# A sliding-window copy: staging whole batches or inner blocks in pairs

## The chip, the cores and the metric

The kernel runs on one core of a Trainium2 chip. The metric is device time in microseconds (us), the median of the timed runs of one program. The kernel before takes 755.48 us, the median of three runs from 754.17 to 756.32. The profiled execution is one more run, with a span of 749.4 us between its first and its last instruction.

## The reference

The kernel computes nothing. It copies overlapping windows of its input.

```python
batch, length, dim = (32, 4096, 256)
window_size = 64
stride = 32

def reference(x, window_size, stride):
    n_windows = (length - window_size) // stride + 1        # 127
    result = np.zeros((batch, n_windows, window_size, dim), dtype=np.float32)
    for i in range(n_windows):
        start = i * stride
        result[:, i] = x[:, start:start + window_size].copy()
    return result
```

A window has twice as many rows as the stride. So it helps to think in *blocks* of 32 rows, 32 x 256 x 4 bytes = 32 KB each. A batch has 128 blocks, and window w is block w followed by block w + 1, that is 64 KB. Block b therefore appears twice in the output: as the first half (half 0) of window b and as the second half (half 1) of window b - 1. Only block 0 and block 127 appear once. The input is 134.2 MB and the output 266.3 MB.

## The kernel before

There are two ways to make a window. A *direct* copy goes from DRAM to DRAM and reads 64 KB for a 64 KB window, so every block is read twice. A *staged* copy loads each block once into on-chip memory (SBUF) and stores it twice. Staging saves reads of DRAM, but moves three blocks' worth of bytes through the DMA engines where direct copying moves two. The kernel uses both at once. SyncE issues direct copies, ScalarE issues loads and stores of staged items, and GpSimd[...] issues remainders near the end.

```python
DIRECT, IN, OUT = 32768, 16384, 16384       # largest piece of a transfer, bytes

class Copier:
    def windows(self, q, b, w0, n, half=None, piece=DIRECT):
        blk = self.blk                       # one block, in elements
        row = [1, 2 * blk if half is None else blk]
        h = half or 0
        return q.dma_start(
            out=self.oap((b * self.nw + w0) * 2 + h, [[2 * blk, n], row]),
            in_=self.xap(b * self.nb + w0 + h, [[blk, n], row]),
            max_dma_last_dim=piece,
        )
    # ... columns: n windows cut into 16 parts each; load, store: blocks to and from a tile

class Staging:                               # cut: __init__ with six tiles of 128 x 32 KB
    def load(self, q, g):
        i = g % len(self.tiles)
        b, c, n = self.items[g]
        if self.count[self.stored[i]]:
            q.wait_ge(self.stored[i], self.count[self.stored[i]])
        step = 128 // n
        parts = [(k, 4, 32, 1) for k in range(4)] if g == 0 else [(0, step, n, step)]
        for rows in parts:
            self.issue(self.c.load(q, self.tiles[i], b, c, rows), self.loaded[i])
        # ...
    def store(self, q, g):
        # ... waits for loaded[i]; one store of all 128 blocks for half 0, one for half 1
        parts, end = [((0, step, n, step), 0), ((0, step, n, step), 1)], []
        # ... the last item is cut into smaller stores, counted in `ended`
    def run(self, q):                        # six loads, six stores, five loads, five stores
        # ...
```

The eleven staged items are whole batches of 128 blocks, one block to a partition. A store of such an item for half 1 puts block 0 of batch b into the second half of the last window of batch b - 1, where it doesn't belong, and a store for half 0 puts block 127 into the first half of a window of the next batch. The direct copies of the neighbouring batches write these places again. They have to come later, so those *edges* wait for the staged stores.

```python
    staged = [*range(1, B, 3)]
    items = [(b, -1 if b == B - 1 else 0, c.nb) for b in staged]
    direct = [b for b in range(B) if b not in staged]
    # ...
    sixteens = []
    for b in direct:
        w = 15 if b - 1 in staged else 0
        sixteens += [(b, w + 16 * j) for j in range((c.nw - w) // 16)]
    edges = [(b, 0 if b - 1 in staged else 112, 15) for b in direct[:-1]]
    last = B - 2
    edges.append((last, 112, 4))

    first_loads, loads, stores = 6 * 17, 5 * 17, 6 * 34
    turns = share = 0
    with tc.tile_critical():
        st.run(ring_s)
        for i, (b, w) in enumerate(sixteens):
            # ...
            second = turns - first_loads - stores
            loading = turns < first_loads or 0 <= second < loads
            share += 120 if turns < 16 or -8 <= second < 16 else 90 if loading else 18
            if share >= 120:                 # one transfer of 16 windows as two of 16 halves
                share -= 120
                turns += 4
                count(c.windows(ring_d, b, w, 16, 0), done)
                count(c.windows(ring_d, b, w, 16, 1), sem)
            else:
                turns += 3
                count(c.windows(ring_d, b, w, 16), sem)
        # ...
        ring_r.wait_ge(near, 16)
        for b, w, n in edges:
            for k in (b - 1, b + 1):
                if k in place and b != last:
                    st.wait_stored(ring_r, place[k])
            count(c.windows(ring_r, b, w, n), rest)
        # ... the last windows, cut in columns, and the waits for everything
```

The variable `turns` counts packets and completions per DMA engine. A transfer of 16 windows gives each of 16 engines one window of 64 KB, which is two pieces of 32 KB and a completion, 3 turns. In two halves it is 4 turns. With `share` the code sets how many turns the SyncE ring has against the ScalarE ring.

Of the kernel before, what the change touches and what calls it, by code (L numbers as in the profile page):

```python
# [8 lines left out]
DIRECT, IN, OUT = 32768, 16384, 16384  # L9


class Copier:


    def __init__(self, x, out, B, L, D, W, S, n_win):
        assert W == 2 * S and L % S == 0
        self.x, self.out = x, out
        self.B = B
        self.blk = S * D
        self.nb = L // S  # L20
        self.nw = n_win

    def xap(self, block, dims):
        return bass.AP(self.x.tensor, self.x.offset + block * self.blk, dims)

    def oap(self, half_window, dims):
        return bass.AP(self.out.tensor, self.out.offset + half_window * self.blk, dims)

    def windows(self, q, b, w0, n, half=None, piece=DIRECT):

        blk = self.blk
        row = [1, 2 * blk if half is None else blk]
        h = half or 0
        return q.dma_start(  # L34
            out=self.oap((b * self.nw + w0) * 2 + h, [[2 * blk, n], row]),
            in_=self.xap(b * self.nb + w0 + h, [[blk, n], row]),
            max_dma_last_dim=piece,
        )

    def columns(self, q, b, w0, n):  # L40

        part = self.blk // 8
        row = [1, part]
        return q.dma_start(  # L44
            out=self.oap((b * self.nw + w0) * 2, [[part, 16], [2 * self.blk, n], row]),
            in_=self.xap(b * self.nb + w0, [[part, 16], [self.blk, n], row]),
        )

    def load(self, q, t, b, c, rows):

        p, step, n, unit = rows
        return q.dma_start(
            out=t[p : p + (n - 1) * step + 1 : step, :],
            in_=self.xap(b * self.nb + c + p // unit, [[step // unit * self.blk, n], [1, self.blk]]),
            max_dma_last_dim=IN,
        )

    def store(self, q, t, b, c, rows, half):


        p, step, n, unit = rows
        w = b * self.nw + c + p // unit - half
        return q.dma_start(
            out=self.oap(2 * w + half, [[2 * step // unit * self.blk, n], [1, self.blk]]),
            in_=t[p : p + (n - 1) * step + 1 : step, :],
            max_dma_last_dim=OUT,
        )


class Staging:  # L70


    def __init__(self, c, tc, pool, dtype, items, bufs):
        self.c, self.items = c, items
        self.tiles = [pool.tile([128, c.blk], dtype, name=f"xb{i}") for i in range(bufs)]
        self.loaded = [tc.alloc_semaphore(f"loaded{i}") for i in range(bufs)]
        self.stored = [tc.alloc_semaphore(f"stored{i}") for i in range(bufs)]
        self.ended = tc.alloc_semaphore("ended")
        self.count = {sem: 0 for sem in (*self.loaded, *self.stored, self.ended)}
        self.after_load, self.after_store = {}, {}  # L80

    def issue(self, dma, sem):
        dma.then_inc(sem, 16)
# [1 line left out]

    def load(self, q, g):
        i = g % len(self.tiles)
        b, c, n = self.items[g]
        if self.count[self.stored[i]]:
            q.wait_ge(self.stored[i], self.count[self.stored[i]])  # L90
        step = 128 // n
        parts = [(k, 4, 32, 1) for k in range(4)] if g == 0 else [(0, step, n, step)]
        for rows in parts:
            self.issue(self.c.load(q, self.tiles[i], b, c, rows), self.loaded[i])
        self.after_load[g] = self.count[self.loaded[i]]

    def store(self, q, g):
        i = g % len(self.tiles)
        b, c, n = self.items[g]
        q.wait_ge(self.loaded[i], self.after_load[g])  # L100
        step = 128 // n
        parts, end = [((0, step, n, step), 0), ((0, step, n, step), 1)], []
        if g == len(self.items) - 1:

            parts = [((0, 1, 128, 1), 1), ((0, 1, 32, 1), 0)]
            end = [(96, 1, 32, 1)] + [(32 + k, 4, 16, 1) for k in range(4)]
        for rows, half in parts:
            self.issue(self.c.store(q, self.tiles[i], b, c, rows, half), self.stored[i])
        for rows in end:
            self.issue(self.c.store(q, self.tiles[i], b, c, rows, 0), self.ended)  # L110
        self.after_store[g] = self.count[self.stored[i]]

    def wait_stored(self, q, g):
        q.wait_ge(self.stored[g % len(self.tiles)], self.after_store[g])  # L114

    def run(self, q):
        bufs = len(self.tiles)
        for first in range(0, len(self.items), bufs):
            group = range(first, min(first + bufs, len(self.items)))
            for g in group:  # L120
                self.load(q, g)
            for g in group:
                self.store(q, g)


@with_exitstack
def kernel(
    ctx: ExitStack,
    tc: tile.TileContext,
    x: bass.AP,  # L130
    window_size: bass.AP,
    stride: bass.AP,
    out: bass.AP,
):
    nc = tc.nc
    W, S = int(window_size), int(stride)
    B, L, D = x.shape
    n_win = (L - W) // S + 1
    assert out.shape == (B, n_win, W, D)
    c = Copier(x, out, B, L, D, W, S, n_win)  # L140


    staged = [*range(1, B, 3)]
    items = [(b, -1 if b == B - 1 else 0, c.nb) for b in staged]
    place = {b: g for g, (b, _, n) in enumerate(items) if n == c.nb}
    direct = [b for b in range(B) if b not in staged]
    pool = ctx.enter_context(tc.tile_pool(name="xb", bufs=1))
    st = Staging(c, tc, pool, x.dtype, items, 6)
    ring_d, ring_s, ring_r = nc.sync, nc.scalar, nc.gpsimd
    done = tc.alloc_semaphore("done")  # L150
    near = tc.alloc_semaphore("near")
    rest = tc.alloc_semaphore("rest")
    total = {done: 0, near: 0, rest: 0}

    def count(dma, sem):
        dma.then_inc(sem, 16)
        total[sem] += 16

    sixteens = []
    for b in direct:
        w = 15 if b - 1 in staged else 0
        sixteens += [(b, w + 16 * j) for j in range((c.nw - w) // 16)]
    singles = [(B - 1, c.nw - 1, 1)]
    edges = [(b, 0 if b - 1 in staged else 112, 15) for b in direct[:-1]]
    last = B - 2
    edges.append((last, 112, 4))

    first_loads, loads, stores = 6 * 17, 5 * 17, 6 * 34  # L170
    turns = share = 0
    with tc.tile_critical():  # L172
        st.run(ring_s)

        for i, (b, w) in enumerate(sixteens):
            sem = near if i == len(sixteens) - 2 else done
            second = turns - first_loads - stores
            loading = turns < first_loads or 0 <= second < loads
            share += 120 if turns < 16 or -8 <= second < 16 else 90 if loading else 18
            if share >= 120:  # L180
                share -= 120
                turns += 4
                count(c.windows(ring_d, b, w, 16, 0), done)
                count(c.windows(ring_d, b, w, 16, 1), sem)
            else:
                turns += 3
                count(c.windows(ring_d, b, w, 16), sem)
            if i == len(sixteens) // 2:
                for b, w, half in singles:
                    count(c.windows(ring_d, b, w, 1, half, 2048), done)  # L190

        ring_r.wait_ge(near, 16)
        for b, w, n in edges:
            for k in (b - 1, b + 1):
                if k in place and b != last:
                    st.wait_stored(ring_r, place[k])
            count(c.windows(ring_r, b, w, n), rest)


        count(c.columns(ring_r, last, 116, 9), rest)  # L200
        st.wait_stored(ring_d, place[B - 1])
        count(c.columns(ring_d, last, 125, 2), done)
        total[st.ended] = st.count[st.ended]
        for sem, n in total.items():
            ring_d.wait_ge(sem, n)


# [33 lines left out]
```

## Time and profile before

| | before |
|---|---|
| time, median of 3 (us) | 755.48 |
| span of the profiled execution (us) | 749.4 |
| loads issued by ScalarE | 10 of 4096 KB, 4 of 1024 KB |
| stores issued by ScalarE | 21 of 4096 KB, 2 of 1024 KB, 4 of 512 KB |
| direct copies issued by SyncE | 92 of 1024 KB, 110 of 512 KB, 1 of 128 KB, 1 of 32 KB |
| direct copies issued by GpSimd | 20 of 960 KB, 1 of 576 KB, 1 of 256 KB |
| median from issue to landing, SyncE's 1024 KB copies (us) | 100.7 |
| median from issue to landing, ScalarE's 4096 KB stores (us) | 139.7 |

The profile of such a kernel is read from its DMA side. A row of 40 slices shows how busy the sixteen DMA engines were in each fortieth of the span (a digit is tenths, 9 is 90% or more) and how many GB/s they moved. A table of queues gives each ring's packets, bytes and the share of the sixteen engines' time that its packets took. Stretches of the span can also be asked for one by one. The long times from issue to landing are no latency of the hardware: a transfer is issued while others still stand ahead of it on its ring.

### The profile page before, as it was taken

The page shows a single profiled execution, that of the slowest core. Times are in us where ns is not written, and L with a number is a line of the kernel's source. Part 1 is how long each engine was busy: PE and PEld are TensorE (multiplying, and loading weights), DVE is VectorE, ACT ScalarE, POOL GpSimd, SP SyncE. Part 2 cuts the span into 40 slices and gives each one's busy share as a digit, 9 for nine tenths or more (in the row PEclk, how much of TensorE's full clock was granted, in tenths as well). Part 3 has the DMA queues.
Part 4 walks back from the last instruction along what each step waited for, and adds up shares of the span by engine and source line. Part 5 has one row for each costly group of instructions (what it writes and reads, how often), then busy time and mean ns, then how long its engine had stood idle before and what let it go on. Part 6 is the DMA issues. An engine that isn't in the chain of part 4 may idle for free.

```text
span 749.4 us, 322 instructions
## 1 busy us (share of the span) xinstructions
POOL 12.8 (2%) x26
## 2 busy tenths in 40 slices
POOL 0000000000000000000000000000000000040100
DMA  8999999999999999999999999999999999999996
GB/s 360 401 427 429 427 429 428 434 423 418 420 424 423 418 424 415 422 427 427 414 427 417 429 432 429 430 422 430 429 423 421 423 421 419 425 426 423 431 409 262
DMA packets 18290, 313.26 MB, mean 418 GB/s; under 512 B 4336, under 2 KB 4336, under 8 KB 4528
## 3 DMA queue, kind: packets, MB, share of 16 engines
q1 hardware_dynamic: 8016, 154.32, 48.8%
q10 hardware_dynamic: 9104, 138.41, 44.0%
q0 software_dynamic: 1168, 20.51, 6.5%
q14 instruction: 2, 0.02, 0.0%
HBM read 220.95 MB, written 267.09 MB: 651 GB/s over the span
## 4 chain that ended last, share of the span: by engine, by line
another core or an unknown queue 92%; POOL 2%; issue 0%; POOLq 0%; SPq 0%
POOL out_dram L34 2%; POOL out_dram L44 0%; POOLq L236 0%; SPq L172 0%; POOLq L114 0%
## 5 line engine op out<-in xcount | busy, mean ns | idle before, releaser
L34 POOL DMA_DIRECT2D out_dram<-in_x_dram x21 | 12.0, 576 | 691.3 <-DMA out_dram<-in_x_dram 654.0
L44 POOL DMA_DIRECT2D out_dram<-in_x_dram x1 | 0.6, 581 | 0.0
L222 POOL MEMSET const-float32-0.0<- 128x1 f32 x1 | 0.1, 98 | 0.2 <-issue 0.2
L222 POOL MEMSET const-bfloat16-1.0<- 128x1 bf16 x1 | 0.1, 101 | 0.0
L222 POOL MEMSET const-float32-1.0<- 128x1 f32 x1 | 0.1, 98 | 0.0
L222 POOL MEMSET const-uint8-127<- 128x1 uint8 x1 | 0.1, 98 | 0.0
## 6 DMA issues: line engine op xcount, KB each, us to landing
out_dram<-in_x_dram SPq DMA_DIRECT2D x92, 1024.0 KB, 100.7
out_dram<-xb ACTq DMA_DIRECT2D x21, 4096.0 KB, 139.7
out_dram<-in_x_dram SPq DMA_DIRECT2D x110, 512.0 KB, 90.3
xb<-in_x_dram ACTq DMA_DIRECT2D x10, 4096.0 KB, 131.4
out_dram<-in_x_dram POOLq DMA_DIRECT2D x20, 960.0 KB, 38.5
xb<-in_x_dram ACTq DMA_DIRECT2D x4, 1024.0 KB, 15.7
out_dram<-xb ACTq DMA_DIRECT2D x2, 1024.0 KB, 113.4
out_dram<-xb ACTq DMA_DIRECT2D x4, 512.0 KB, 96.9
```

The lines of the kernel that those rows point to most:

```text
L34: return q.dma_start(out=self.oap((b * self.nw + w0) * 2 + h, [[2 * blk, n], row]), in_=self.xap(b * self.nb + w0 + h, [[blk, n], row]), m ...
L44: return q.dma_start(out=self.oap((b * self.nw + w0) * 2, [[part, 16], [2 * self.blk, n], row]), in_=self.xap(b * self.nb + w0, [[part, 16 ...
L222: nc = _bacc.Bacc("TRN2", target_bir_lowering=False, num_devices=1)
```

## The change

The staged items no longer are whole batches. An item is now blocks 1 to 64 of two batches that lie 16 apart, one on the even and one on the odd partitions of a tile. Eleven items cover 22 batches. Their stores fill exactly the second halves of windows 0 to 63 and the first halves of windows 1 to 64, so nothing is written that has to be written again, and no direct copy waits for a staged store. Each item takes two loads and four stores in place of one and two.

What remains is cut so that every transfer has 16 rows. Windows 65 to 112 of all batches go in three transfers of 16 windows per batch (`whole`). The inner parts of the ten batches that aren't staged go as pairs of half-window transfers (`split`). Windows 113 to 126, and the halves left over in windows 0 and 64, go by a new kind of transfer (`across`): one window of 16 batches at a time, whose rows lie a batch apart. All of these are on the SyncE ring; GpSimd's software ring is gone. The constants of `share` are set anew for the changed turns.

```diff
-    def columns(self, q, b, w0, n):
-        ...
+    def across(self, q, b, w, half=None):
+
+        blk = self.blk
+        row = [1, 2 * blk if half is None else blk]
+        h = half or 0
+        return q.dma_start(
+            out=self.oap(b, w, h, [[2 * self.nw * blk, 16], row]),
+            in_=self.xap(b, w + h, [[self.nb * blk, 16], row]),
+            max_dma_last_dim=DIRECT,
+        )
 ...
-        step = 128 // n
-        parts = [(k, 4, 32, 1) for k in range(4)] if g == 0 else [(0, step, n, step)]
-        for rows in parts:
-            self.issue(self.c.load(q, self.tiles[i], b, c, rows), self.loaded[i])
+        b, far, c, n = self.items[g]
+        step = 4 if g == 0 else 2
+        for k in range(step):
+            dma = self.c.load(q, self.tiles[i], b + far * (k % 2), c + k // 2, k, step, 2 * n // step)
+            self.issue(dma, self.loaded[i])
 ...
+        b, far, c, n = self.items[g]
+        for half in (0, 1):
+            for k in (0, 1):
+                self.issue(self.c.store(q, self.tiles[i], b + far * k, c, k, n, half), self.stored[i])
 ...
-    staged = [*range(1, B, 3)]
-    items = [(b, -1 if b == B - 1 else 0, c.nb) for b in staged]
+    far, pairs, n = B // 2, 11, 64
+    items = [(g, far, 1, n) for g in range(pairs)]
 ...
+    whole, split, cross = [], [], []
+    for b in range(B):
+        whole += [(b, w) for w in range(n + 1, n + 49, 16)]
+        if b % far >= pairs:
+            split += [(b, w) for w in range(0, n, 16)]
+    for w in range(n + 49, n_win):
+        cross += [(b, w) for b in (0, far)]
+    where = len(whole) // 4
+    jobs = [("whole", *k) for k in whole[:where]]
+    jobs += [("cross", *k) for k in cross]
+    jobs += [("whole", *k) for k in whole[where:]]
 
-    first_loads, loads, stores = 6 * 17, 5 * 17, 6 * 34
+    first_loads, loads, stores = 6 * 18, 5 * 18, 6 * 36
 ...
-            share += 120 if turns < 16 or -8 <= second < 16 else 90 if loading else 18
+            share += 120 if turns < 16 or -8 <= second < 16 else 100 if loading else 52
 ...
+            if split and (halves or k == len(jobs)):
+                b, w = split.pop(0)
+                turns += 4
+                count(c.windows(ring_d, b, w, 1))
+                count(c.windows(ring_d, b, w + 1, 0))
+                continue
 ...
+            if k == len(jobs) // 2:
+                for b in (0, far):
+                    turns += 4
+                    count(c.across(ring_d, b, 0, 0))
+                    count(c.across(ring_d, b, n, 1))
 
-        ring_r.wait_ge(near, 16)
-        for b, w, n in edges:
-            ...
-        count(c.columns(ring_r, last, 116, 9), rest)
-        st.wait_stored(ring_d, place[B - 1])
-        count(c.columns(ring_d, last, 125, 2), done)
+        ring_d.wait_ge(done, total)
+        st.wait_all(ring_d)
```

## The prediction

> **What bounds the kernel now.** No engine computes: section 1 of the page has only GpSimd, busy for 12.8 us of 749.4. So I read the DMA side: first the row of slices, then the queues.
>
> ```profile
> DMA  8999999999999999999999999999999999999996
> GB/s 360 401 427 429 427 429 428 434 423 418 420 424 423 418 424 415 422 427 427 414 427 417 429 432 429 430 422 430 429 423 421 423 421 419 425 426 423 431 409 262
> DMA packets 18290, 313.26 MB, mean 418 GB/s; under 512 B 4336, under 2 KB 4336, under 8 KB 4528
> ## 3 DMA queue, kind: packets, MB, share of 16 engines
> q1 hardware_dynamic: 8016, 154.32, 48.8%
> q10 hardware_dynamic: 9104, 138.41, 44.0%
> q0 software_dynamic: 1168, 20.51, 6.5%
> HBM read 220.95 MB, written 267.09 MB: 651 GB/s over the span
> ```
>
> q1 is the SyncE ring (DRAM to DRAM), q10 the ScalarE ring (staging through SBUF), q0 the GpSimd software ring. The shares add to 99.3%: the sixteen engines are full from the second slice to the last but one. A byte also costs the same on each: 48.8% of 749.4 us is 365.7 us for 154.32 MB, 422 GB/s; q10 gives 138.41 MB in 329.7 us, 420 GB/s; q0 20.51 MB in 48.7 us, 421 GB/s. The time is bytes moved over about 421 GB/s, plus a start and an end. Bytes per stage come from the stretches (columns: stretch, length, GpSimd busy, clock, DMA share, GB/s):
>
> ```profile
> 2.00:28.00 26.00, 0.00 (x0) 1.00 0.99 397
> 28.00:45.00 17.00, 0.00 (x0) 1.00 1.01 422
> 45.00:130.00 85.00, 0.00 (x0) 1.00 1.01 428
> 150.00:350.00 200.00, 0.00 (x0) 1.00 1.00 422
> 500.00:650.00 150.00, 0.00 (x0) 1.00 1.01 424
> 660.00:735.00 75.00, 6.95 (x13) 1.00 1.01 420
> 735.00:742.00 7.00, 0.00 (x0) 1.00 0.95 397
> 742.00:750.00 8.00, 0.00 (x0) 1.00 0.15 62
> ```
>
> Loading stages (45 to 130) run at 428, storing stages at 422 to 424, the stage with the software ring (660 to 735) at 420. The end is sharp: 397 until 742 us, then nearly nothing. What is left to win lies in bytes, in 2% of rate, and in a few us at the two ends.
>
> The waits list shows one more thing:
>
> ```profile
> POOL out_dram L34 <- DMA out_dram<-in_x_dram: 654.0, 1, 654.0
> POOL out_dram L34 <- DMA out_dram<-xb: 37.4, 1, 37.4
> ```
>
> GpSimd waits 654 us by design and once 37.4 us for a staged store, before its last edges. In that time the engines moved 420 GB/s from other rings, so the wait costs nothing.
>
> **What the Trainium skill says.** Its page "DMA: Bandwidth & Descriptors" bears on three points. "Why a DMA increments its semaphore by 16 and not by 1": a transfer uses the largest number of engines up to 16 that divides the slowest dimension of both sides. Every transfer of the new kernel has 16, 32 or 64 rows, so each loads the sixteen engines alike; the old 15-window edges do not divide so. No view of before names the engines of a transfer. "Queues, rings and completion order": an engine goes round robin over its rings, packet by packet. The profile agrees: packets per engine are 9104/16 = 569 on q10 and (8016 + 1168)/16 = 574 on the other two, and both ended together. "Latency and other measured facts": copies of 16 KiB rows ran at 207 GB/s per direction with rows 512 KiB apart, 164 at 2 MiB and 103 at 4 and 8 MiB. No transfer of the kernel before takes its slowest dimension over batches; the new one reads rows 4 MiB apart. "SBUF — State Buffer", "Door 1: The DMA port swizzle", says partitions 0 to 63 reach only half of the ports; rows interleaved over 128 partitions, as here, reach all. The first item of before is loaded in such strided quarters, and 2 to 28 us ran at 397, but that holds the start too, so it is weak evidence of a small cost.
>
> **The change part by part.**
>
> Staging. Before: loads 10 x 4096 + 4 x 1024 KB = 44 MiB, stores 21 x 4096 + 2 x 1024 + 4 x 512 KB = 88 MiB, together the 138.41 MB of q10. After: eleven items of 2 x 64 blocks of 32 KB, 44 MiB in and, each block going to two windows, 88 MiB out. The same: 0 us.
>
> Direct bytes. The output is 32 x 127 x 64 KB = 266.34 MB; staging gives 92.27, so 174.06 MB are direct, against 154.32 + 20.51 = 174.83. This 0.77 MB is what was stored twice (HBM written says it too: 267.09 against 266.34). At 421 GB/s: -1.8 us.
>
> Transfers and their completions. Before issues 41 on ScalarE's ring, 204 on SyncE's, 22 on GpSimd's. After, by its own loop: ScalarE 24 loads and 44 stores; SyncE 53 whole transfers, 71 in two halves, 40 split pairs, 4 half columns: 279. So 80 more completion packets on each engine. No view prices one; 4336 small packets already fit in shares that account for the whole span at one rate per byte, so I allow +0.7 us.
>
> Balance. Packets with completions per engine: ScalarE 11 x (18 + 36) + 2 = 596; SyncE, counting as the code does, 593. The rings should end together, as 569 and 574 do now. 0 us.
>
> Software ring. Its stage at 420 instead of 424 GB/s over 75 us is 0.7 us; the ragged end (397 for 7 us) is 0.4 us. Both go: -1.1 us. GpSimd's 12.6 us of issuing were beside other work.
>
> HBM evenness. The new loop halves more transfers in the storing stages (52 of 120 against 18), so SyncE's share there falls and with it the HBM traffic per byte moved. Storing is the slower stage, 422 against 428; a quarter of that 1.4% over some 520 us is about -1.8 us. This is a guess at size.
>
> Columns over batches. Windows 113 to 126, 28 transfers of 1 MiB, plus 4 of 0.5 MiB: 31.5 MB in all. In the code's count the 28 lie at turns 228 to 329 of 593, all in the first storing stage (turns 108 to 324), about 100/593 of 745 us = 127 us. Their writes are 8 MiB minus 64 KB apart, which is not a power of two; only the reads alias. If the halving that the skill's page states held in full, the 29.4 MB, 70 us of the sixteen engines at 421 GB/s, would take 140: +70 us. Three things speak against the full size: rows here are 64 KB, not 16; only one side of the copy has the pitch; and staged packets run between. So my weights are 45% nothing (0 to 2 us), 30% a mild cost (3 to 15 us), 25% a large one (20 to 70 us). Median about +4 us.
>
> Sum: 755.5 - 1.8 + 0.7 - 1.1 - 1.8 + 4 = 755.5. The columns are the one uncertain part that is not small, and they can only cost, so I set 756.
>
> **The rivals.**
>
> *Aliased reads become the bound of a stage.* For: the skill's measurement, and HBM already moves 651 GB/s on average, so an uneven spread has little slack. The author put the columns into a storing stage, away from the staged loads, which looks like caution. Against: the three points above. It makes 775 to 825 us.
>
> *Strided partitions slow the staging.* Every load and store now takes each second partition. For: 397 GB/s at the start. Against: the start also holds first latencies, and 413 to 469 GB/s appear inside it (5 to 15 us in 5-us stretches). If each staged stage fell by 2%, the time would be 768.
>
> *The change wins more than bytes.* Half-empty engines from the 15-window edges, if any, and uneven storing would come back: at 428 GB/s throughout, 312.5 MB take 730 us, and with the 12.4 us that now lie outside (749.4 less 313.26 MB at 425, 737.1) it is 742 in the span, some 748 in the timed runs, which lie 6 us above the span. Faster by 2%, below 740, would need a rate that no long stretch of before has shown.
>
> **Range and chances.** With no pitch effect the parts give 748 to 753; with a mild one 753 to 766; with a large one 770 and more. A range of 746 to 780 leaves a tenth on either side. Faster by over 2% (under 740.4) 0.04; slower by over 2% (over 770.6) 0.24, which is the large pitch effect and a little of the strided partitions; within 2% 0.72.
>
> **What would show it.** The queues of the changed kernel should read 138.41 MB on q10, 174.06 on q1, none on q0, HBM written 266.34 MB. The slices should stay at 420 to 430 with 9s to the end. The columns should be visible, or not, between about 285 and 420 us, shortly after the quarter of the whole transfers: GB/s well under 420 there with the DMA share still at 1.0 means aliased reads. If the loss lies in all storing slices, it is the strided partitions. If the last slice falls below 262 with one queue alone, the balance of turns was wrong. The prediction fails mainly if the pitch cost is large, or if storing runs at 430, which would make it 745 or less.

## The result, and the profile after

The changed kernel takes 816.53 us (median of 6 runs, 814.34 to 821.31), the kernel before beside it 755.66. The ratio is 1.082, with a 95% interval of 1.078 to 1.086. The prediction was 756 us, with a range of 746 to 780; the result is 37 us above the range.

These lines of the page of the changed kernel answer to those shown of before, slices first and then queues.

```profile
DMA  8999999999999999999999999999999999999995
GB/s 366 417 425 425 418 415 430 425 419 416 427 413 415 401 317 282 273 261 283 280 269 272 274 403 428 411 418 419 427 421 417 413 419 418 420 414 417 421 413 251
DMA packets 19026, 312.51 MB, mean 381 GB/s; under 512 B 5264, under 2 KB 5264, under 8 KB 5264
## 3 DMA queue, kind: packets, MB, share of 16 engines
q1 hardware_dynamic: 9488, 174.08, 55.5%
q10 hardware_dynamic: 9536, 138.42, 43.8%
HBM read 220.20 MB, written 266.34 MB: 594 GB/s over the span
```

The bytes are what the steps had: 174.08 MB direct, 138.42 staged, 266.34 written. The GB/s row has a trench of nine slices, from the fifteenth to the twenty-third, while the row of busy tenths above it stays at 9. The stretches give its size (columns: stretch, length, GpSimd busy, clock, DMA share, GB/s):

```profile
2.00:275.00 273.00, 0.00 (x0) 1.00 1.01 419
287.00:473.00 186.00, 0.00 (x0) 1.00 1.01 279
475.00:805.00 330.00, 0.00 (x0) 1.00 1.00 419
```

186 us at 279 GB/s move 51.9 MB. At 419 they would take 124 us, so the trench holds 62 us, all of the loss. It begins at 287 us, where the prediction had put the 28 columns over batches (between about 285 and 420 us); a *column* is one transfer of `across`. The queues of this stretch, and below them those of the first storing stage of the kernel before (150 to 350 us), show what became of each ring:

```profile
q1 hardware_dynamic: 1552, 29.36, 57.5%
q10 hardware_dynamic: 1550, 22.56, 43.1%
```

```profile
q1 hardware_dynamic: 2338, 48.30, 57.6%
q10 hardware_dynamic: 2342, 36.01, 42.9%
```

The 29.36 MB on q1 are just what the 28 columns have: 158 GB/s of direct copying, where the kernel before had 242. Both rings passed the same number of packets, so the staging was held to the pace of the columns and fell from 180 to 121 GB/s, although its own transfers were of the same kind as outside the trench.

### The profile page after: what moved, and what is told of

It is laid out like the page before. It is cut to its first block, busy times and chain, and to the rows that moved or that the text cites. A ratio compares the mean times of both kernels' runs of the same rounds, so it can differ in the third digit from the quotient of the medians.

```text
span 819.5 us, 382 instructions
## 1 busy us (share of the span) xinstructions
POOL 0.2 (0%) x4
## 3 DMA queue, kind: packets, MB, share of 16 engines
q1 hardware_dynamic: 9488, 174.08, 55.5%
q10 hardware_dynamic: 9536, 138.42, 43.8%
HBM read 220.20 MB, written 266.34 MB: 594 GB/s over the span
```

## The experiments

Three theories were on the table. A: the sixteen rows of a column lie a multiple of 4 MiB apart, so their reads fall on the same few memory channels at once ("aliased" reads; the channels are the theory's picture, and the runs can test only the distance). B: rows from sixteen batches are slow wherever exactly they lie, perhaps on the writing side. C: strided partitions or the many small transfers cost time. Ratios are to the kernel before, run on the same chip, with 95% intervals in brackets. In experiments 1, 2, 3, 5 and 6 the columns, those for the half windows too, read other rows of the input than the reference asks for, as many bytes as before, and write where they wrote; only the distance of the reads differs.

### 1. Rows 4 MiB + 32 KB apart

```diff
-            in_=self.xap(b, w + h, [[self.nb * blk, 16], row]),
+            in_=self.xap(b, w + h - 15 if w >= 15 else w + h, [[self.nb * blk + blk, 16], row]),
```

> The columns over batches read their sixteen rows 4 MiB + 32 KB apart instead of 4 MiB; everything else, writes too, is as in the changed kernel (the data read for windows 113 to 126 and for the half columns are therefore other rows of the input). Theory A, the sixteen engines read addresses that fall on the same few memory channels because their rows lie a multiple of 4 MiB apart: the stretch at 275 GB/s goes, 420 throughout, 750 to 754 us. Theory B, rows of sixteen different batches are slow wherever exactly they lie, on the reading or the writing side: nothing changes, 812 to 820 us. Theory C, strided partitions or the many small transfers cost time: the slow stretch goes only in part, over 770 us.

754.32 us against 752.56, ratio 1.0023 (1.0009 to 1.0038). The trench is gone but for a shallow rest, which the stretches show:

```profile
150.00:275.00 125.00, 0.00 (x0) 1.00 1.00 422
280.00:440.00 160.00, 0.00 (x0) 1.00 1.01 410
445.00:730.00 285.00, 0.00 (x0) 1.00 1.01 423
```

The rows still come from sixteen batches, the writes are untouched, and the strided partitions and all transfers are there. B and C fall as causes of the loss; the exact distance of the reads is the cause.

### 2, 5 and 6. How far apart is far enough

The same line with 4 KB, 16 KB and 64 KB in place of 32 KB (the start moved back to stay inside the input):

```diff
-            in_=self.xap(b, w + h, [[self.nb * blk, 16], row]),
+            in_=self.xap(b, w + h - 2 if w >= 2 else w + h, [[self.nb * blk + blk // 8, 16], row]),    # 4 KB
+            in_=self.xap(b, w + h - 8 if w >= 8 else w + h, [[self.nb * blk + blk // 2, 16], row]),    # 16 KB
+            in_=self.xap(b, w + h - 30 if w >= 30 else w + h, [[self.nb * blk + 2 * blk, 16], row]),   # 64 KB
```

> As the 32 KB skew, but rows 4 MiB + 4 KB apart, so that the sixteen rows of 64 KB still overlap in their position modulo 4 MiB. Theory A with channels that change every 4 KB or less: 750 to 756 us, the skew need not be as long as a row. If channels change only with 32 KB or more: still slow, about 800 us. Theory B: 812 to 820 us.

> Column rows 4 MiB + 16 KB apart, between the 4 KB skew (796 us, 1.058 of before) and the 32 KB skew (754 us, 1.002). If the loss follows how far the sixteen rows are spread in position modulo 4 MiB (240 KB here, 60 KB and 480 KB there), this lies between them, about 1.01 to 1.03. If the memory changes channel with an address bit of 16 KB or less, it is as good as the 32 KB skew, below 1.006.

> Column rows 4 MiB + 64 KB apart, that is at the distance that rows of 16 windows have on the writing side, plus 4 MiB. If what remains of the loss in the 32 KB skew (about 409 GB/s from 280 to 440 us against 423 around it) is overlap of the 64 KB rows, it goes: 420 there, ratio to before 0.995 to 1.000. If it belongs to columns as such (writes over sixteen batches), it stays: 405 to 412 GB/s, ratio 1.002.

The 4 KB skew (a skew is what the distance has beyond 4 MiB) took 796.42 us, ratio 1.058 (1.055 to 1.061): most of the loss stayed, near the 800 us of the second branch of its expectation. 16 KB: 763.38 us, 1.0115 (1.0095 to 1.0135), inside its expectation. 64 KB: 753.52 us, 0.999 (0.997 to 1.001). The stretches of the three, in this order:

```profile
300.00:350.00 50.00, 0.00 (x0) 1.00 1.01 305
350.00:400.00 50.00, 0.00 (x0) 1.00 1.00 303
```

```profile
280.00:440.00 160.00, 0.00 (x0) 1.00 1.01 395
```

```profile
280.00:440.00 160.00, 0.00 (x0) 1.00 1.01 418
```

So with the sixteen rows spread over 0, 60, 240, 480 and 960 KB of position modulo 4 MiB, the stretch runs at 279, about 304, 395, 410 and 418 GB/s. The last is the rate around it: nothing of the loss belongs to columns as such, and what experiment 1 left went with the larger skew as well. Whether the rows must not overlap, or must only be spread over enough positions, was not told apart: skew and spread grew together, and the columns' rows stayed as long as they were.

### 3. Rows 2 MiB apart

```diff
-            in_=self.xap(b, w + h, [[self.nb * blk, 16], row]),
+            in_=self.xap(b, w + h - 64 if w >= 64 else w + h, [[self.nb * blk // 2, 16], row]),
```

> The columns read rows 2 MiB apart (64 blocks, two rows of each batch), writes as they were. Theory A, after the skill's figures (164 GB/s at 2 MiB between 207 and 103): part of the loss stays, 765 to 795 us, with about 330 GB/s in the stretch. Theory B: eight batches in place of sixteen, 780 to 816 us. An exact 4 MiB effect only: 750 to 756 us.

771.88 us, ratio 1.025 (1.023 to 1.027), in theory A's branch, with a stretch above the 330 GB/s expected:

```profile
300.00:350.00 50.00, 0.00 (x0) 1.00 1.00 356
350.00:400.00 50.00, 0.00 (x0) 1.00 1.01 363
```

Half of the distance costs about a third of the loss. The Trainium skill's page "DMA: Bandwidth & Descriptors", "Latency and other measured facts", has the same order (207 GB/s without aliasing, 164 at 2 MiB, 103 at 4 MiB). Its padding does not carry over as a number: there 4 KiB restored the full rate for 16 KiB rows, here 4 KB brought 279 to some 304 only. But its tile has 128 rows, which 4 KiB of padding spreads over 508 KiB (an estimate from that page's figures), and a column has sixteen, spread over 60 KB. With a spread of 480 KB it ran at 410 here too.

### 4 and 8. The same columns, spread over the run

```diff
-    where = len(whole) // 4
-    jobs = [("whole", *k) for k in whole[:where]]
-    jobs += [("cross", *k) for k in cross]
-    jobs += [("whole", *k) for k in whole[where:]]
+    jobs, put = [], 0
+    for i, k in enumerate(whole):
+        jobs.append(("whole", *k))
+        while put < len(cross) * (i + 1) // len(whole):
+            jobs.append(("cross", *cross[put]))
+            put += 1
```

> The same transfers as in the changed kernel, with the 28 columns spread evenly over the whole run, about one after each three or four transfers within a batch. Theory A as a cap on the rate of the aliased channels, which holds only while most engines are in a column at once: engines that are some us apart are then mostly in other transfers, 752 to 770 us. Theory A as a cost of each aliased row, paid wherever the row stands (2.2 us for each of 28 columns): 810 to 818 us, without a slow stretch but with every slice near 385 GB/s.

781.03 us, ratio 1.0375 (1.035 to 1.040). This is between the two branches: about 45% of the loss stayed. The trench is gone, and the loss is spread:

```profile
GB/s 371 409 428 423 418 425 406 429 390 424 376 392 409 408 400 399 380 397 402 405 397 387 406 418 415 424 402 415 405 405 386 394 411 404 380 401 411 408 396 270
```

In a second version each column was cut into its two halves, which stood one at a time between the others:

```diff
+    pieces = [(b, w, h) for b, w in cross for h in (0, 1)]
 ...
-        while put < len(cross) * (i + 1) // len(whole):
-            jobs.append(("cross", *cross[put]))
+        while put < len(pieces) * (i + 1) // len(whole):
+            jobs.append(("cross", *pieces[put]))
 ...                                                  # a half column counts 2 turns
```

> All outputs as in the changed kernel. Each column is cut into its two halves of 32 KB rows, and the 56 halves stand one at a time between transfers within a batch. Spreading whole columns gave 781 us, 27 above the 754 of the 32 KB skew, out of 60. If what counts is how many engines stand in the same column at a time, rows half as long halve this again: 764 to 770 us. If each aliased byte costs the same once the columns are apart: 778 to 784 us.

779.17 us, 1.033 (1.031 to 1.035). This one is not clean. It has 10160/16 = 635 packets per engine on the SyncE ring against 596 on the other, so that ring was left alone at the end; its last three slices are 387, 325 and 201 GB/s, against 421, 413 and 251 in the changed kernel. Some 8 us of its time are that end (an estimate from these slices of 19.4 us). Before that end the rates, first of whole columns and then of halves, are

```profile
120.00:640.00 520.00, 0.00 (x0) 1.00 1.01 403
120.00:640.00 520.00, 0.00 (x0) 1.00 1.01 411
```

against 420 in the same stretch of the 64 KB skew. The shortfall is about half, as the first branch had it; the time of 779 us is in the second branch, but without the end it would be some 771. Because packets and their order changed too, this is a hint, not a proof. That spreading helps because engines some way apart stand in different transfers is argued; no view names the engines of a transfer.

### 7, 10 and 11. What limits direct copying, and what staging

The first of these leaves the staging out: the windows it would fill stay unwritten, and the SyncE ring makes its 174 MB of direct copies alone.

```diff
 ...                                                  # the tiles of the staging
-        st.run(ring_s)
 ...
-        st.wait_all(ring_d)
```

> Nothing is staged (the windows that staging would fill stay unwritten); the SyncE ring alone makes its 174 MB of direct copies, the columns at 4 MiB as in the changed kernel. If the aliased reads are capped by the memory, columns run at the rate they had beside the staging, about 29.4 MB in 186 us, 160 GB/s (150 to 200), and everything around them above 400. If the cost is a fixed stretching of each packet, by 420/275 = 1.53, columns run at about 275 GB/s. In all about 174 MB: 350 to 370 us plus 20 to 120 us.

One run, 623.41 us, far above what was expected. The columns did what theory A as a cap said, but the transfers around them were slow too:

```profile
20.00:200.00 180.00, 0.00 (x0) 1.00 1.00 328
240.00:380.00 140.00, 0.00 (x0) 1.00 1.00 167
440.00:600.00 160.00, 0.00 (x0) 1.00 1.00 330
```

Columns run at 167 GB/s alone and at 158 beside the staging: it is more like a ceiling for the aliased reads than a fixed stretching of each packet, which would have given 275, or 215 if the same factor is taken from the 328 around the columns. But why only 328 for copies within a batch? Either one ring can't fill the engines, or the memory is at its limit with 328 read and 328 written. The next kernel alternates the same transfers between the SyncE and the ScalarE ring:

```diff
 ...                                                  # no staging, and a semaphore for each ring
             halves = share >= 120
+            ring = ring_d if ring is ring_s else ring_s
 ...                                                  # and ring for ring_d in the transfers
```

> As the run with direct copies alone (which ran at 330 GB/s in transfers within a batch and 167 in the columns), but the transfers alternate between the SyncE and the ScalarE ring. If the memory limits direct copies, at 2 x 330 = 660 GB/s read and written: still 325 to 335 GB/s and 160 to 175 in the columns, 615 to 625 us. If one ring alone cannot keep the engines busy: 400 to 425 GB/s in transfers within a batch, 520 to 560 us.

One run, 609.09 us; stretches:

```profile
20.00:200.00 180.00, 0.00 (x0) 1.00 1.00 329
260.00:340.00 80.00, 0.00 (x0) 1.00 1.01 181
400.00:600.00 200.00, 0.00 (x0) 1.00 1.00 323
```

A second ring changes nothing for copies within a batch, 329 GB/s. The columns, at 181, ran a little above the 160 to 175 expected, and the time ended below 615 us; so the ceiling of aliased reads isn't one fixed figure, and why two rings raise it stays open. The third kernel has the staging alone, with its strided partitions, and leaves all direct copies out:

```diff
-        k = 0
-        while k < len(jobs) or split:
-            ...
-        ring_d.wait_ge(done, total)
         st.wait_all(ring_d)
```

> Only the staging, 46.1 MB of loads and 92.3 MB of stores on the ScalarE ring, with no direct copies (the other windows stay unwritten). If the sixteen engines limit the mix and the strided partitions cost nothing: 420 to 428 GB/s, 330 to 345 us. If the strided partitions or one ring alone are slow: below 400 GB/s.

One run, 330.46 us:

```profile
20.00:310.00 290.00, 0.00 (x0) 1.00 1.01 429
```

So staging alone runs at 429 GB/s, on one ring and with every second partition: theory C has nothing left to stand on there. Direct copying, which loads the memory with two bytes for each byte moved, stops at 329, that is 658 GB/s of memory traffic. The storing stage of before, by the queues shown above, has 2 x 48.30 + 36.01 MB in 200 us, 663 GB/s. If packets follow one another on an engine, a fixed time for each direct packet is ruled out: the 174.8 MB direct and 138.4 MB staged of before would take 531 + 323 us at the two rates, and took 749. That a shared limit of the memory makes the 329 is inferred from this, from the agreement and from the two rings; no run measured the memory in another way. The skill's page "HBM Reference", "Specifications (TRN2)", gives about 716 GB/s for the domain of two cores, which no long stretch here reached.

### 9 and 12. The pairs kept, the columns undone

All outputs are as in the reference. Windows 113 to 126 go as 32 transfers of 14 windows of one batch on the GpSimd ring, and the four half columns stand apart.

```diff
+        row = [1, 2 * self.blk]                       # a new method, tail
+        return q.dma_start(
+            out=self.oap(b, w, 0, [[2 * self.blk, n], row]),
+            in_=self.xap(b, w, [[self.blk, n], row]),
 ...
-            ... 100 if loading else 52
+            ... 100 if loading else 68
 ...
+        ring_r.wait_ge(near, 16)                      # the last whole transfer but two
+        for b in range(B):
+            c.tail(ring_r, b, n + 49, n_win - n - 49).then_inc(rest, 16)
```

> Undoes the one part that is suspected and keeps the rest: the pairs of inner blocks stay staged, windows 113 to 126 go as 32 transfers of 14 windows of one batch on the GpSimd software ring, which starts when the SyncE ring is nearly done; the four half columns stand apart from each other, and the share in the storing stages is 68 for 52, for rings that end together. Nothing is stored twice and all outputs are as the reference has them. Theory A: no slow stretch, 750 to 755 us, 0.993 to 0.999 of before (0.8 MB less than before, and no waits for staged stores). If the software ring costs what was gained: 1.000 to 1.005. If the pairs themselves cost (theory C): above 1.01.

755.10 us against 751.88, ratio 1.0046 (1.0027 to 1.0065). The trench is gone, but the gain over the kernel before did not come. Its rings ended apart: 8128/16 + 1536/16 = 604 packets per engine against 596 (taken as even over the engines, which no view shows). From 735 us on the GpSimd ring was nearly alone, with 2.79 of the 3.17 MB, and the rate fell:

```profile
735.00:742.00 7.00, 0.00 (x0) 1.00 0.97 351
```

The last kernel sets that share back from 68 to 52, for 593 packets against 596.

> As the software ring for the 14-window remainders, with one number changed: the share in the storing stages is 52 again instead of 68, which takes 11 packets from each engine on the SyncE ring (497 for 508). With the 96 of the software ring, as its run counted them, that is 593 against 596 on the ScalarE ring; before it was 604. If the 0.5% by which that run was above the kernel before is the direct ring left alone at the end (351 GB/s from 735 to 742 us and a last slice of 207), the end is full again: 2 to 4 us less, 0.998 to 1.002. If it lies in the many small transfers or in the pairs, the ratio stays 1.003 to 1.006.

753.45 us against 751.07, ratio 1.0033 (1.0017 to 1.0048): inside the branch that puts the rest elsewhere, but its interval and that of the run with 68 overlap, so what the end was worth is not settled. The end is filled to 742 us, as before, and the long stretches are a little slower than those of before (422, 424 and 420 there):

```profile
150.00:350.00 200.00, 0.00 (x0) 1.00 1.01 420
500.00:650.00 150.00, 18.51 (x32) 1.00 1.01 423
660.00:735.00 75.00, 0.00 (x0) 1.00 1.00 417
735.00:742.00 7.00, 0.00 (x0) 1.00 0.94 391
```

What makes this 0.3% was not told apart: the 737 more packets could, and so could the four half columns, which still read 4 MiB apart (2.1 MB; at the 62 us for 29.36 MB they would cost some 4 us, an estimate). None of the runs that write all windows as the reference has them beat the kernel before.

## Why the prediction was wrong

*What bounds the kernel now.* The step read full engines as the limit, because a byte cost the same on all three rings. That sign cannot tell: in the trench, where the columns are the slow part, 57.5% of 186 us for 29.36 MB is 275 GB/s, and 43.1% for the 22.56 MB of staging is 281, nearly the same price. Nor can the share of 1.00, which stands over 429 GB/s of staging, 329 of direct copies and 167 of columns: engines held packets, but it doesn't say what they waited for. In the mix both limits nearly meet: 422 to 428 GB/s where staging alone makes 429, and 663 GB/s of memory traffic in a storing stage, if 658 is about the memory's limit.

*Bytes, balance, completions.* 174.08 and 138.42 MB, 266.34 MB written, and 593 and 596 packets per engine (9488/16 and 9536/16) are what the steps said. The count of transfers was not. The step had 53 transfers whole and 71 in halves; it is the other way round, as the page shows (71 of 1024 KB, 190 of 512):

```profile
out_dram<-in_x_dram SPq DMA_DIRECT2D x190, 512.0 KB, 91.5
out_dram<-in_x_dram SPq DMA_DIRECT2D x71, 1024.0 KB, 91.9
```

That is 261 transfers for 279, so 62 completions more per engine instead of 80, which would lower the +0.7 us by a fifth or so.

*Columns over batches.* This is the step that failed, by its cost and not by its mechanism. It worked out +70 us for the full halving, then gave a large cost a quarter of the chances and put +4 us into the sum. Measured are 62 us. Each of the three reasons for the discount fell. "Rows here are 64 KB, not 16": the halving came in full, from 328 GB/s to 167 in direct copies alone. "Only one side of the copy has the pitch": moving the reads alone removed the loss, so the reads alone made it. "Staged packets run between": columns run at 158 GB/s with staged packets between and at 167 without, and the staged packets, passing one for one with those of the columns, fell to 121 GB/s themselves. The mechanism stood among the rivals with its right range, "775 to 825 us", and the right sign to look for, a dip with the DMA share at 1.0 from about 285 us; its chance was too small.

*The small gains.* Bytes -1.8, software ring -1.1, evenness -1.8 and completions +0.7 make -4.0 us, 0.995 of before. The 64 KB skew, which has all of them and no aliasing, is at 0.999 (0.997 to 1.001): they came to a fifth or so of that, by the interval to little more than half at most, if to anything. The evenness did not show: from 150 to 350 and from 500 to 650 us that kernel ran at 419 and 421 GB/s, where before had 422 and 424. Why is open.

*Strided partitions.* The rival's 768 us did not happen: staging alone ran at 429 GB/s, and the 64 KB skew, with all the strided transfers in it, took what before took.

## What to carry to other kernels

Before choosing the slow dimension of a transfer, take the distance of its rows on each side; where it is a multiple of 2 or 4 MiB, as here, shift the rows or leave the dimension inside one stretch of memory. Here a shift by the row length, 64 KB, was enough and 4 KB was not; other lengths and numbers of rows were not tried. A full DMA share does not say whether engines or memory are the limit; run each kind of traffic alone to see. And a published measurement of the very pattern outweighs a handful of reasons why this case should be milder, until one of those reasons has been measured.

## What the runs showed of the hardware that was not expected

- Copies from DRAM to DRAM within a batch run at 329 GB/s, on one ring or on two, staging through SBUF at 429. The mix of before reaches 418 in the mean, more than the 366 that sharing the engines' time at these two rates would give; that the two use different limits is the reading that fits.
- With rows 4 MiB apart on the reading side alone, direct copies run at 167 GB/s on one ring and 181 on two. At 2 MiB the mix runs at about 360 GB/s where it would run at 420.
- Spreading aliased transfers through the run about halved their cost (from 1.082 to 1.0375), with as many transfers of each size.
- Two rings with work passed packets one for one (1552 and 1550 in the trench), so slow packets on one held the other to 121 GB/s, where the kernel before had 180.
